# First products of a latent attention: weights split one item ahead, both blocks rotated in one operation, the keys' common part on GpSimd, another order

## The chip, the cores and the metric

The kernel runs on one core of a Trainium2 chip. The metric is the device time of one execution in microseconds. The core's engines work side by side, each through its own queue in order: TensorE (PE, with its weight loads as PEld), VectorE (DVE), ScalarE (ACT), GpSimd (POOL) and SyncE (SP), which here only issues transfers. Semaphores order the engines among each other.

## The reference, cut to what matters

The program is a two-layer block of mixers, cross attention and MLPs on a sequence of 256 tokens with 1024 features, followed by a second block: a latent attention, an expert stage (64 experts), a pool mixer and a second expert stage. The change lies in the latent attention (and in a few lines at the head of the expert stages):

```python
def mla_mixer(x, cos, sin, w_in, q_norm, w_uq, kv_norm, w_ukv, w_o):
    lat = x @ w_in                                         # 256 + 128 + 32 columns
    c_q = rms_norm(lat[..., :Q_LORA_RANK], q_norm)
    c_kv = rms_norm(lat[..., Q_LORA_RANK:Q_LORA_RANK + KV_LORA_RANK], kv_norm)
    k_rope = apply_rope(lat[..., Q_LORA_RANK + KV_LORA_RANK:], cos, sin)
    q = (c_q @ w_uq).reshape(B, S, N_HEADS, QK_NOPE_DIM + QK_ROPE_DIM)   # 16 heads, 64 + 32
    q_nope = q[..., :QK_NOPE_DIM]
    q_rope = apply_rope(q[..., QK_NOPE_DIM:], cos[:, :, None, :], sin[:, :, None, :])
    kv = (c_kv @ w_ukv).reshape(B, S, N_HEADS, QK_NOPE_DIM + V_HEAD_DIM)
    k_nope, v = kv[..., :QK_NOPE_DIM], kv[..., QK_NOPE_DIM:]
    # causal softmax attention of q_nope, q_rope on k_nope, k_rope, then
    return o @ w_o
```

The rotation of each head's 32 columns is x1*cos - x2*sin and x2*cos + x1*sin on halves of 16. The keys have one rotated part for all heads.

## The kernel before, in words

**Weights.** All weights come through one list of items in the order of use, 1 MB or a little less each. `issue` (L170 to L188) starts a transfer into the next slot of a ring of ten; SyncE issues it, eight early items of the expert stage go through GpSimd's queue. In the expert stages thirteen more slots come in. The products of the first half work in a split form: `split_steps` (L225 to L241) has ScalarE copy an item's high part (`wh`, L236) and VectorE subtract to get the low part (`wl`, L239), in two halves, and both take slots of the same ring. A product with a split weight is three matmul passes: (high, high), (low weight, high), (high, low input). `w(key)` (L243 to L251) hands out the next item and decides how far ahead items are split and issued at that point; `tick` splits one half of an item where the program calls it. The items of the latent attention are lat0, lat1, uq0, ukv0, uq1 and the output weights mo0 to mo3.

**The latent attention, `mla`.** Tokens lie in two blocks of 128 (`b`). The order on every engine is the order in which the program is written. First the latent product (PE, L285), the evacuation `lat` with the row scale (ACT, L1170), transposes (PE, L1175), the transposed latents' high part `cTh` (ACT, L1177) and low part `cTl` (DVE, L1178), sums of squares (ACT, L1182), the inverse root of four columns on VectorE (L1184, L373 to L377: one start, three rounds) giving `rr`, and the scale of the queries `rqs` (DVE, L1188). Then `rope` (L1198 to L1209), six operations on VectorE for one block: for the keys' common part (`kr`, copied into `ka`, `kb`, `kc` at L1232) and at the end of `uq(i)` for eight heads of queries. `uq(i)` (L1211 to L1224) is 24 matmuls into four PSUM banks, which ScalarE evacuates with `rqs` (L1221). `ukv(j)` (L1236 to L1246) is the product for four heads' keys and values: keys evacuated by ScalarE (L1245), values by VectorE (L1246). `pre(p)` transposes queries and keys of two heads (PE, L1255) and copies them out, one head on VectorE (L1258), one on ScalarE (L1260). `scores(p)` (L1266, L1267) and the softmax (row bound on VectorE L443, exponential on ScalarE L455, normalization on VectorE L463, L467) follow; `att.main` runs the pairs of heads with the output product (L322).

**What stands between.** After the first two pairs' scores, `bc(10)` (L1032) broadcasts a gain vector through TensorE into two PSUM banks, VectorE multiplies x by row scale and gain (L1293, four operations of 128x512), the output weights mo0 are split by four ticks, and `uq(1)` follows. The product with x into the accumulator (L1300) opens the main loop. `moe` begins with copies of the accumulator into x (ACT L1363, DVE L1364), with statistics (L1366, L1371) for the norm.

## Time and profile before

| what | value |
|---|---|
| time, median of 3 runs | 1840.31 us (1839.34 to 1840.73) |
| the profiled execution's own time | 1839.08 us |
| its span | 1837.3 us |
| mean granted TensorE clock | 0.960 |
| TensorE busy | 1645.4 us (90%) |
| VectorE busy | 763.4 us (42%) |
| ScalarE busy | 576.6 us (31%) |
| GpSimd busy | 12.5 us (1%), 27 instructions |
| moved by DMA | 550.11 MB, 299 GB/s over the span |

The page cuts the span into 40 slices of 46 us. The latent attention lies in slices 18 and 19; the expert stages and the pool mixer are the slices behind it. In the timeline a row is a start, a duration, an engine, a line, the operation with its operands and shape; an `x4` behind it groups four consecutive ones, with their summed time; in brackets stands how long the engine was idle before and what released it.

### The profile page before, as it was taken

The numbers are of one execution on the slowest core, as the hardware profiler recorded it, in microseconds if no ns is written. First come the engines' busy times: TensorE is split into PE (matmuls) and PEld (weight loads), VectorE is DVE, ScalarE is ACT, GpSimd is POOL, SyncE is SP. The second block draws the span as 40 slices with busy tenths as digits, with TensorE's granted clock in tenths as the row PEclk, the third lists the DMA queues.
The fourth block names the chain that finished last, engine by engine and source line by source line (L and its number), as shares of the span: only waits on it lengthen the run. The fifth ranks groups of instructions, "written<-read, shape, count | busy, mean of one in ns | idle before, by whom it ended". The sixth has DMA issues, their size and how long they took to land.

```text
span 1837.3 us, 29848 instructions
## 1 busy us (share of the span) xinstructions
PE 1645.4 (90%) x12682; PEld 1200.0 (65%) x12682; DVE 763.4 (42%) x1582; ACT 576.6 (31%) x1043; POOL 12.5 (1%) x27
## 2 busy tenths in 40 slices
PE   7999999999999999999998778878799977987876
PEld 7998899999878899987754344434366434443433
DVE  6886476555676565568521121111043202110102
ACT  5545454444465454456411100000022100000001
POOL 0000000000000000000000000000000000000000
PEclk9999999999999999999999988988999998988899
DMA  8543455555534355546899999999999999999996
GB/s 299 177 161 116 131 175 198 184 185 181 184 115 136 118 186 189 192 151 248 319 416 426 426 426 425 426 426 426 420 426 425 426 426 426 426 424 426 426 426 255
DMA packets 128902, 550.11 MB, mean 299 GB/s; under 512 B 10891, under 2 KB 32883, under 8 KB 80499
## 3 DMA queue, kind: packets, MB, share of 16 engines
q1 hardware_dynamic: 127107, 539.27, 75.0%
q0 software_dynamic: 1216, 8.39, 1.2%
q8 instruction: 103, 1.69, 0.3%
q10 hardware_dynamic: 432, 0.39, 0.1%
q14 instruction: 44, 0.36, 0.1%
HBM read 546.98 MB, written 1.05 MB: 298 GB/s over the span
## 4 chain that ended last, share of the span: by engine, by line
PE 50%; DMA 45%; DVE 3%; ACT 2%; issue 1%; SPq 0%; ACTq 0%; DVEq 0%
DMA wr<-in_moe_w 44%; PE a L322 16%; PE b L306 9%; PE a L306 6%; PE a L285 3%; PE b L763 3%; PE a L763 2%; PE b L1497 2%; PE b L486 1%; PE b L1465 1%; PE b L475 1%; PE b L346 1%; PE b L801 1%; DMA wr<-in_xa_w_kv 1%; PE b L734 1%; PE b L828 1%
## 5 line engine op out<-in xcount | busy, mean ns | idle before, releaser
L1497 PE MATMUL b<-wr,xg 128*32 128x256 f32 x4096 | 307.0, 426 | 107.9 <-DMA wr<-in_moe_w 107.9
L239 DVE TENSOR_TENSOR wl<-wr,wh 128x1024 fp32r<-128x1024 f32 (+4 forms) x268 | 309.8, 1198 | 115.3 <-ACT wh L236 67.6
L1497 PEld LDWEIGHTS b<-wr,xg 128*32 128x32 f32 x4096 | 148.9, 122 | 272.9 <-DMA wr<-in_moe_w 146.4
L236 ACT ACTIVATE wh<-wr 128x1024 fp32r<-128x1024 f32 (+4 forms) x268 | 265.1, 1037 | 99.9 <-DVE wl L239 72.0
L1501 DVE SCALAR_TENSOR_TENSOR th<-th,b 128x256 f32<-128x256 f32 x32 | 13.5, 421 | 482.3 <-ACT th L1500 482.3
L1500 ACT ACTIVATE th<-b 128x256 f32<-128x256 f32 x32 | 12.3, 384 | 520.8 <-PE b L1497 520.8
L322 PE MATMUL a<-wh,yh 128*128 128x512 f32 x416 | 169.0, 406 | 0.0
L322 PE MATMUL a<-wh,yl 128*128 128x512 f32 x416 | 164.6, 396 | 0.6 <-DVE yl L337 0.6
L322 PE MATMUL a<-wl,yh 128*128 128x512 f32 x416 | 164.0, 394 | 0.0
L1465 PE MATMUL b<-G,x 128*128 128x128 f32 x1024 | 132.3, 290 | 19.4 <-DVE G L1447 10.5
L1524 PE MATMUL b<-wr,hT 128*32 128x512 f32 x992 | 124.7, 601 | 27.7 <-ACT hT L1512 23.2
L1465 PEld LDWEIGHTS b<-G,x 128*128 128x128 f32 x1024 | 126.0, 204 | 32.9 <-issue 17.3
L306 PE MATMUL b<-xh,wl 128*128 128x256 f32 x448 | 121.9, 282 | 0.0
L306 PE MATMUL b<-xh,wh 128*128 128x256 f32 x448 | 121.8, 281 | 0.0
L1533 PE MATMUL a<-Y,GT 128*128 128x512 f32 x248 | 116.9, 614 | 0.0
L306 PE MATMUL b<-xl,wh 128*128 128x256 f32 x448 | 110.4, 282 | 0.0
L1524 PEld LDWEIGHTS b<-wr,hT 128*32 128x32 f32 x992 | 32.7, 110 | 99.0 <-issue 51.2
L322 PEld LDWEIGHTS a<-wh,yl 128*128 128x128 f32 x416 | 78.1, 188 | 20.2 <-DVE yl L337 1.4
L1533 PEld LDWEIGHTS a<-Y,GT 128*128 128x128 f32 x248 | 42.0, 189 | 75.2 <-issue 29.7
L322 PEld LDWEIGHTS a<-wh,yh 128*128 128x128 f32 x416 | 78.1, 188 | 19.7 <-issue 3.0
L322 PEld LDWEIGHTS a<-wl,yh 128*128 128x128 f32 x416 | 78.3, 188 | 17.1
L306 PE MATMUL a<-xh,wh 128*128 128x256 f32 x320 | 88.8, 287 | 0.1
(467 smaller groups left out, 2468.9 us busy)
## 6 DMA issues: line engine op xcount, KB each, us to landing
wr<-in_moe_w SPq DMA_DIRECT2D x368, 1024.0 KB, 19.6
wr<-in_mlp_w_up SPq DMA_DIRECT2D x32, 1024.0 KB, 5.3
wr<-in_mlp_w_down SPq DMA_DIRECT2D x32, 1024.0 KB, 4.8
wr<-in_xa_w_kv SPq DMA_DIRECT2D x16, 1024.0 KB, 5.8
wr<-in_xa_w_q SPq DMA_DIRECT2D x8, 1024.0 KB, 5.0
wr<-in_xa_w_o SPq DMA_DIRECT2D x8, 1024.0 KB, 4.8
wr<-in_cd_w_in SPq DMA_DIRECT2D x8, 1024.0 KB, 5.0
wr<-in_moe_w POOLq DMA_DIRECT2D x8, 1024.0 KB, 6.6
```

Source lines behind the costliest of these rows:

```text
L236: nc.scalar.activation(hi[:, s], r[:, s], AF.Copy)
L239: nc.vector.tensor_tensor(lo[:, s], r[:, s], hi[:, s].bitcast(F32), op=ALU.subtract)
L285: nc.tensor.matmul(outs[b][j], xT(a, h * 4 + kk)[:, b * 128:(b + 1) * 128], wt[c][:, kk, j * n:(j + 1) * n], start=(h == 0 and kk == 0 and ...
L306: nc.tensor.matmul(o[f // 2][:, f % 2, :], wt[c][:, kk, f * 128:(f + 1) * 128], xT(a, h * 4 + kk), start=(h == 0 and kk == 0 and a == 0 an ...
L322: nc.tensor.matmul(acc[b][hf], yT[a][:, chunk, b * 128:(b + 1) * 128], wt[c][:, j, hf * 512:(hf + 1) * 512], start=(first and a == 0 and c ...
L346: nc.tensor.transpose(ps[k // 2][:, k % 2, b * 128:(b + 1) * 128], x[:, b, k * 128:(k + 1) * 128], self.ident)
L475: nc.tensor.transpose(ps[:, o:o + 128], s[:, o:o + 128], self.ident)
L763: nc.tensor.matmul(o[:, f], lt, rt, start=(k == 0 and f == 0 and a == 0 and c == 0), stop=(k == 7 and c == 1), skip_group_check=True)
L1465: nc.tensor.matmul(ps[:, k], xk[:, b, 4 * i + k], Gf[:, b], start=(b == 0), stop=(b == 1))
L1497: nc.tensor.matmul(ps[32 * e:32 * e + 32, which], xg[:, k, 32 * e:32 * e + 32], w(e, k), start=(which == 0 and k == 0), stop=(k == 7), ski ...
L1524: nc.tensor.matmul(y[hf][32 * e:32 * e + 32], hT[:, c, 32 * e:32 * e + 32], w(c)[:, hf * 512:(hf + 1) * 512], start=(c == 0), stop=(c == 1 ...
L1533: nc.tensor.matmul(acc[b][hf], GT[:, b * 128:(b + 1) * 128], Y[:, hf * 512:(hf + 1) * 512], start=first, stop=end, skip_group_check=True)
```

## The change

The diff touches five places. `w()` splits one item less far ahead at lat1 and uq0, finishes an item that is half split when it is asked for, and issues one transfer less at one point. In `mla`, the gain broadcast moves right behind the evacuation of the latents, and the multiplication of x between the inverse root and the query scale. `rope` takes an engine and both blocks at once, 256 elements per partition for eight heads; the keys' part runs on GpSimd, and the queries' rotation becomes `turned_q(i)`, called after `ukv(0)` and after `uq(1)`. The values of the second block are evacuated by ScalarE. The products are called in another order, the four ticks stand once before and once behind `uq(1)`. In `moe` the first statistics stand behind both copies.

```diff
--- before.py
+++ after.py
@@ -245,9 +245,11 @@
         assert self.items[i][0] == key, (self.items[i][0], key)
         self.w_next += 1
         if self.w_split <= i or not self.attending:
-            self.split(i + (0 if i == 0 else 1 if i < 3 else 3 if key == ("lat", 1) else 2))
+            self.split(i + (0 if i == 0 else 1 if i < 3 or key in (("lat", 1), ("uq", 0)) else 2))
+        elif self.part is not None and self.w_split == i + 1:
+            self.split(i)
         left = self.n_split - i
-        self.issue(self.n_split + {4: 3, 3: 4, 2: 5, 1: 7}[left] if left < 5 else i + 2 + self.depth)
+        self.issue(self.n_split + {4: 3, 3: 4, 2: 5, 1: 7}[left] if left < 5 else i + 2 + self.depth - (left == 6))
         return self.sp.pop(i)
 
     def step(self):
@@ -1168,6 +1170,7 @@
             lat = ap.tile([128, 2, 416], F32, name="lat")
             for b in range(2):
                 nc.scalar.activation(lat[:, b], o[b][0], AF.Copy, scale=rs[:, b:b + 1])
+            gain = self.bc(10)
             cT = [ap.tile([128, 3, 256], F32R, name=n) for n in ("cTh", "cTl")]
             for c in range(3):
                 ps = self.pb([128, 256])
@@ -1184,6 +1187,11 @@
                 nc.vector.tensor_scalar(t, t, 1.0 / n, 1e-6, op0=ALU.mult, op1=ALU.add)
             self.rsqrt(rr, 4)
             rk = rr[:, 2:4]
+
+            for b in range(2):
+                for h in range(2):
+                    t = x[:, b, h * 512:(h + 1) * 512]
+                    nc.vector.scalar_tensor_tensor(t, t, rs[:, b:b + 1], gain[h], op0=ALU.mult, op1=ALU.mult)
             rqs = ap.tile([128, 2], F32, name="rqs")
             nc.vector.tensor_scalar(rqs, rr[:, 0:2], -(96.0 ** -0.5), None, op0=ALU.mult)
 
@@ -1195,18 +1203,23 @@
             qk = [ap.tile([96, 2, 256], F32, name=f"qkT{i}") for i in range(4)]
             va, vb = ap.tile([128, 2, 8, 64], F32, name="va"), ap.tile([128, 2, 4, 64], F32, name="vb")
 
-            def rope(dst, src, nh, b):
-                x1, x2 = src[:, :, 0:16], src[:, :, 16:32]
-                cos = cs[:, 0, b, None, :].to_broadcast([128, nh, 16])
-                sin = cs[:, 1, b, None, :].to_broadcast([128, nh, 16])
-                t = self.cc(C_SWA, 256).rearrange("p (h d) -> p h d", d=32)[:, :nh]
-                u = ru[:, :nh]
-                nc.vector.tensor_tensor(t[:, :, 0:16], x1, cos, op=ALU.mult)
-                nc.vector.tensor_tensor(t[:, :, 16:32], x2, cos, op=ALU.mult)
-                nc.vector.tensor_tensor(u[:, :, 0:16], x2, sin, op=ALU.mult)
-                nc.vector.tensor_tensor(u[:, :, 16:32], x1, sin, op=ALU.mult)
-                nc.vector.tensor_tensor(dst[:, :, 0:16], t[:, :, 0:16], u[:, :, 0:16], op=ALU.subtract)
-                nc.vector.tensor_tensor(dst[:, :, 16:32], t[:, :, 16:32], u[:, :, 16:32], op=ALU.add)
+            def rope(eng, dst, src, t, u):
+
+                nh = src.shape[2]
+                x1, x2 = src[:, :, :, 0:16], src[:, :, :, 16:32]
+                cos, sin = (cs[:, i, :, None, :].to_broadcast([128, 2, nh, 16]) for i in range(2))
+                eng.tensor_tensor(t[:, :, :, 0:16], x1, cos, op=ALU.mult)
+                eng.tensor_tensor(t[:, :, :, 16:32], x2, cos, op=ALU.mult)
+                eng.tensor_tensor(u[:, :, :, 0:16], x2, sin, op=ALU.mult)
+                eng.tensor_tensor(u[:, :, :, 16:32], x1, sin, op=ALU.mult)
+                eng.tensor_tensor(dst[:, :, :, 0:16], t[:, :, :, 0:16], u[:, :, :, 0:16], op=ALU.subtract)
+                eng.tensor_tensor(dst[:, :, :, 16:32], t[:, :, :, 16:32], u[:, :, :, 16:32], op=ALU.add)
+
+
+            kr, kt_, ku_ = (ap.tile([128, 2, 1, 32], F32, name=n) for n in ("kr", "krt", "kru"))
+            rope(nc.gpsimd, kr, lat[:, :, None, 384:416], kt_, ku_)
+            for k, n in ((ka, 8), (kb, 4), (kc, 4)):
+                nc.gpsimd.tensor_copy(k[:, :, :, 64:96], kr.to_broadcast([128, 2, n, 32]))
 
             def uq(i):
                 wt = self.w("uq", i)
@@ -1219,18 +1232,13 @@
                                                  start=(k == 0 and a == 0 and c == 0), stop=(k == 1 and a == 1))
                         h = 8 * i + 4 * j
                         nc.scalar.activation(qt[h // 4][:, b].rearrange("p h d -> p (h d)"), o, AF.Copy, scale=rqs[:, b:b + 1])
-                for b in range(2):
-                    t = (qa, qb)[i][:, b, :, 64:96]
-                    rope(t, t, 8, b)
-            ru = ap.tile([128, 8, 32], F32, name="ru")
+
+            def turned_q(i):
+                t = (qa, qb)[i][:, :, :, 64:96]
+                rope(nc.vector, t, t, *ru)
+            ru = [ap.tile([128, 2, 8, 32], F32, name=n) for n in ("rt", "ru")]
             vc = ap.tile([128, 2, 4, 64], F32, name="vc")
             v = [(va, 0), (va, 4), (vb, 0), (vc, 0)]
-            for b in range(2):
-                t = ap.tile([128, 1, 32], F32, name="kr", bufs=2)
-                rope(t, lat[:, b, None, 384:416], 1, b)
-                for k, n in ((ka, 8), (kb, 4), (kc, 4)):
-                    nc.vector.tensor_copy(k[:, b, :, 64:96], t.to_broadcast([128, n, 32]))
-
             uq(0)
             self.attend_on()
             wt = self.w("ukv", 0)
@@ -1243,7 +1251,11 @@
                                          start=(a == 0 and c == 0), stop=(a == 1))
                     ov = o.rearrange("p (h d) -> p h d", d=128)
                     nc.scalar.activation(kt[j][:, b, :, 0:64], ov[:, :, 0:64], AF.Copy, scale=rk[:, b:b + 1])
-                    nc.vector.tensor_scalar(v[j][0][:, b, v[j][1]:v[j][1] + 4], ov[:, :, 64:128], rk[:, b:b + 1], None, op0=ALU.mult)
+                    vd = v[j][0][:, b, v[j][1]:v[j][1] + 4]
+                    if b:
+                        nc.scalar.activation(vd, ov[:, :, 64:128], AF.Copy, scale=rk[:, b:b + 1])
+                    else:
+                        nc.vector.tensor_scalar(vd, ov[:, :, 64:128], rk[:, b:b + 1], None, op0=ALU.mult)
             QK = {}
 
             def pre(p):
@@ -1277,23 +1289,21 @@
             att = self.attend(ap, 8, scores, lambda h, kb: v[h // 4][0][:, kb, v[h // 4][1] + h % 4], lambda h: mask, outp,
                                     lambda p: (ys[p // 4][0][:, p % 4], ys[p // 4][1][:, p % 4]), pre=pre)
             ukv(0)
+            turned_q(0)
             ukv(1)
+            ukv(2)
             pre(0)
-            ukv(2)
+            ukv(3)
             pre(1)
-            ukv(3)
             att.pro(0)
             att.pro(1)
             att.soft2(0)
-
-            g = self.bc(10)
-            for b in range(2):
-                for h in range(2):
-                    t = x[:, b, h * 512:(h + 1) * 512]
-                    nc.vector.scalar_tensor_tensor(t, t, rs[:, b:b + 1], g[h], op0=ALU.mult, op1=ALU.mult)
             for _ in range(4):
                 self.tick()
             uq(1)
+            turned_q(1)
+            for _ in range(4):
+                self.tick()
             acc = self.pacc()
             for b in range(2):
                 for h in range(2):
@@ -1362,12 +1372,10 @@
         for b in range(2):
             nc.scalar.activation(half_x(b, 0), by8(y[b][0]), AF.Copy)
             nc.vector.tensor_copy(half_x(b, 1), by8(y[b][1]))
-            if b == 0:
-                nc.vector.bn_stats(st[:, 0, 0], y[0][0])
         for b in range(2):
             for k in range(8):
                 nc.tensor.transpose(pt[b][k // 4][:, k % 4], xk[:, b, k], self.ident)
-        for b, h in ((0, 1), (1, 0), (1, 1)):
+        for b, h in ((0, 0), (0, 1), (1, 0), (1, 1)):
             nc.vector.bn_stats(st[:, b, h], y[b][h])
         for b in range(2):
             for i in range(2):
```

VectorE's queue from the end of the inverse root (`rr` is its result, `rqs` the scale of the queries, `kr` the keys' rotated part, `qa` the first eight heads of queries, `cst`, `ru` and `rt` room for the rotation). Before:

```order
L377 SCALAR_TENSOR_TENSOR rr<-nwt,nwy 128x4
L1188 TENSOR_SCALAR rqs<-rr 128x2
L1204 TENSOR_TENSOR cst<-lat,cs 128x16
L1205 TENSOR_TENSOR cst<-lat,cs 128x16
L1206 TENSOR_TENSOR ru<-lat,cs 128x16
L1207 TENSOR_TENSOR ru<-lat,cs 128x16
L1208 TENSOR_TENSOR kr<-cst,ru 128x16
L1209 TENSOR_TENSOR kr<-cst,ru 128x16
L1232 COPY ka<-kr 128x8x32
L1232 COPY kb<-kr 128x4x32
L1232 COPY kc<-kr 128x4x32
```

The same place in the changed kernel:

```order
L379 SCALAR_TENSOR_TENSOR rr<-nwt,nwy 128x4
L1194 SCALAR_TENSOR_TENSOR x<-x,rs,b 128x512 x4
L1196 TENSOR_SCALAR rqs<-rr 128x2
L239 TENSOR_TENSOR wl<-wr,wh 128x1024 x2
L1258 TENSOR_SCALAR va<-a,rr 128x256
L1211 TENSOR_TENSOR rt<-qa,cs 128x16x16
L1212 TENSOR_TENSOR rt<-qa,cs 128x16x16
L1213 TENSOR_TENSOR ru<-qa,cs 128x16x16
L1214 TENSOR_TENSOR ru<-qa,cs 128x16x16
L1215 TENSOR_TENSOR qa<-rt,ru 128x16x16
L1216 TENSOR_TENSOR qa<-rt,ru 128x16x16
```

The multiplications of x now stand ahead of the scale, the low halves of the key/value weights behind it, and the keys' rotation is gone from this queue.

ScalarE's queue around the second query product, from the last exponential of the first pairs (`qb` the second eight heads of queries, `pt` transposed probabilities). Before:

```order
L455 ACTIVATE s,den<-s,mn 128x256
L1260 ACTIVATE qkT_7896<-b 96x512
L236 ACTIVATE wh<-wr 128x1024 x2
L1221 ACTIVATE qb<-a,rqs 128x384 x4
L477 ACTIVATE pt<-b 128x384 x2
```

The same place in the changed kernel:

```order
L457 ACTIVATE s,den<-s,mn 128x256
L1272 ACTIVATE qkT_7898<-b 96x512
L236 ACTIVATE wh<-wr 128x768 x2
L1234 ACTIVATE qb<-a,rqs 128x384 x4
L236 ACTIVATE wh<-wr 128x1024 x2
L479 ACTIVATE pt<-b 128x384 x2
```

The halves of 1024, the output weights mo0, moved behind the query evacuation; in their place stand halves of 768, the weights of the second query product itself.

## Rows read from the trace of the kernel before

**Rows 1.** The page's rate strip: GB/s in 40 equal slices of the span.
```profile
GB/s 299 177 161 116 131 175 198 184 185 181 184 115 136 118 186 189 192 151 248 319 416 426 426 426 425 426 426 426 420 426 425 426 426 426 426 424 426 426 426 255
```

**Rows 2.** Windows: span, length, busy us of PE, PEld, DVE, ACT, POOL, clock, DMA, GB/s.
```profile
840.00:860.00 20.00, 19.77 (x124) 16.30 (x123) 17.95 (x68) 15.04 (x45) 1.06 (x2) 1.00 0.64 258
860.00:880.00 20.00, 20.00 (x127) 15.91 (x126) 13.35 (x49) 13.78 (x42) 1.06 (x2) 1.00 0.32 115
880.00:900.00 20.00, 20.00 (x115) 14.86 (x114) 9.29 (x27) 10.09 (x24) 1.31 (x4) 1.00 0.90 349
```

**Rows 3.** Timeline of the transfer issues on SyncE's and GpSimd's queues: start, us, queue, operation.
```profile
899.71 3.50 SPq L182 DMA_DIRECT2D wr<-in_moe_w  x7
...
822.45 1.09 POOL L182 DMA_DIRECT2D wr<-in_moe_w  x2 [355.96 <-ACT wh L236]
```

**Rows 4.** Waits of PE from 820 to 860: us in total, times, longest.
```profile
PE b L1255 <- DVE qa L1209: 1.0, 1, 1.0
PE b L1175 <- ACT lat L1170: 0.9, 2, 0.8
PE a L1218 <- DVE cTl L1178: 0.8, 1, 0.8
```

**Rows 5.** Timeline around the second query product (L1218).
```profile
842.07 1.95 PE L1032 MATMUL b<-brow,keep 128*128 128x128 f32 x16
...
843.77 0.42 PE L1218 MATMUL a<-wh,cTh 128*128 128x384 f32 x1
...
844.00 2.72 DVE L1293 SCALAR_TENSOR_TENSOR x<-x,rs,b 128x512 f32<-128x512 f32 x4
844.00 1.99 ACT L236 ACTIVATE wh<-wr 128x1024 fp32r<-128x1024 f32 x2
```

**Rows 6.** Timeline of the first products, from the splits to the queries' rotation.
```profile
821.05 4.10 DVE L239 TENSOR_TENSOR wl<-wr,wh 128x1024 fp32r<-128x1024 f32 x4
...
823.70 1.20 ACT L1177 ACTIVATE cTh<-b,col 128x256 fp32r<-128x256 f32 x3 [0.42 <-PE b L1175]
...
828.92 0.17 DVE L1188 TENSOR_SCALAR rqs<-rr 128x2 f32<-128x2 f32 x1
...
829.18 2.00 ACT L1221 ACTIVATE qa<-a,rqs 128x384 f32<-128x384 f32 x4 [2.47 <-DVE rqs L1188]
...
829.82 0.50 PE L1242 MATMUL a<-wh,cTh 128*128 128x512 f32 x1
...
831.30 0.29 DVE L1204 TENSOR_TENSOR cst<-qa,cs 128x128 f32<-128x128 f32 x1
```

**Rows 7.** Timeline: TensorE's first head transposes.
```profile
834.11 0.32 PE L1255 MATMUL b<-keep,qa 128*96 128x128 f32 x1 [0.96 <-DVE qa L1209]
```

**Rows 8.** Chain of waits, 805 to 905: the third key/value product's piece (start, us).
```profile
835.09 1.38 PE a L1242 x6
```

**Rows 9.** Timeline: the product with x, and VectorE's copy behind the second normalization.
```profile
848.07 3.59 PE L1300 MATMUL a<-x,keep 128*128 128x512 f32 x8
...
853.23 0.69 DVE L1258 COPY qkT<-b 96x512 f32<-96x512 f32 x1 [0.44 <-PE b L1255]
```

**Rows 10.** Groups by line on GpSimd: busy us, mean ns of one.
```profile
L1735 POOL TENSOR_TENSOR Y<-Y,x 128x512 f32<-128x512 f32 x2 | 3.2, 1592 | 480.0 <-ACT Y L1733 479.9
L1360 POOL TENSOR_SCALAR r_i<-keep 128x32 f32<-128x32 f32 x4 | 1.2, 289 | 0.2
```

**Rows 11.** Timeline: the first statistics of the expert stage.
```profile
899.77 0.70 DVE L1366 BATCH_NORM_STATS2 n_st<-a 128x6 f32<-128x512 f32 x1 [0.15 <-PE a L322]
```

**Rows 12.** Timeline: TensorE after a wait in the first mixer.
```profile
39.31 0.39 PE L285 MATMUL a<-wh,xh 128*128 128x260 f32 x1 [3.13 <-DVE gate L573]
```

**Rows 13.** Windows behind that wait, columns as in rows 2.
```profile
39.50:40.00 0.50, 0.29 (x2) 0.09 (x1) 0.50 (x2) 0.50 (x2) 0.00 (x0) 0.68 1.11 354
40.00:41.00 1.00, 1.00 (x5) 1.00 (x6) 0.93 (x3) 1.00 (x4) 0.00 (x0) 0.50 1.10 346
...
44.00:45.00 1.00, 0.00 (x0) 0.00 (x0) 1.00 (x4) 1.00 (x2) 0.00 (x0) 1.00 0.60 125
```

## The prediction

> **What bounds the kernel now.** I began with the page's strip of rates over the span. From about the twentieth of its 40 slices the memory side moves some 426 GB/s without a break [rows 1]. So the second half (the two expert stages) is bound by transfers; what happens before it counts by when it lets those transfers start. The busy table by stretches answers that: from 860 to 880 us TensorE is busy for 20.00 of 20 us while the DMA share is 0.32, and from 880 to 900 it has risen to 0.90 [rows 2]. The issue list says what it waits for: seven weight items go out together at 899.71 [rows 3], the moment at which the latent attention frees its ring slots. Until then the ring is full, after it the DMA share never drops. **A microsecond added to the latent attention before 899.7 therefore reaches the end nearly whole**, as does one saved.
>
> Inside that stage TensorE waits little: 1.0 us for the rotated queries, 0.9 for the evacuated latents, 0.8 for the low half of the transposed latents [rows 4]. These three are the whole of its waits there, so little can be won. The changed lines sit between 821 and 859 us.
>
> **The change part by part.** All sums are on the profiled execution, 1839.08 us, whose span is 1837.3; the median of the three runs, 1840.31, is 1.23 above it, and I add that at the end.
>
> *Front (821 to 829).* The gain broadcast moves from before the second query product to right behind the latent product. There it ran from 842.07 to the next product at 843.77, 1.70 us [rows 5]. Put at 821.91, when the latent product is through, it ends at 823.6. The transposes start behind it; two of them, some 0.5 us, lie ahead of ScalarE's first copy of them, which today starts at 823.70 [rows 6] and becomes 824.1. Most of the broadcast hides under the latents' evacuation; **0.4 us sticks out**. The VectorE's four low-half operations (4.10 us from 821.05 [rows 6]: two of 1024 and two of 768 elements, so 1.17 and 0.88 us each) are no longer there, because the splits now run one item ahead. That removes the 0.8 wait for the low half. But the first query product ends the same 0.5 us earlier and meets the next wait, so nothing of it reaches the end.
>
> *The scale of the queries.* Now to the step that decides. VectorE's queue held: inverse root, query scale (828.92), key rotation, query rotation from 831.30 [rows 6]. It will hold: inverse root, the four multiplications of x by its gain, query scale. These four took 2.72 us [rows 5]. They used to stand where VectorE had time; now ScalarE's four query evacuations, which already wait 2.47 us for the scale [rows 6], wait for them too. The scale comes 0.4 + 2.72, less a small overlap, **3.04 us later**, at 831.96. TensorE cannot go round it: the first key/value product takes a PSUM bank that the first evacuation frees (it started 0.90 behind the scale, at 829.82 [rows 6]), so it starts at 832.86, and TensorE, finished with the queries at 829.2, stands still for **3.6 us**.
>
> *Rotation.* Twelve operations of 128 elements at a spacing of 0.20 us become six of 256. Their shape is not in the trace. The spacing cannot be under 0.20 nor over 0.40 (no saving); between 16 elements and 128 an operation grows by about 1.07 ns per element (0.29 us at 128 [rows 6]), which gives 0.334, and I take 2.17 us with the first latency, against 2.6 now. With the two low halves of the key/value weights (2.34 us) and a value copy ahead of it in the queue, the rotation ends at 837.36. The head transposes, today at 834.11 behind a wait of 0.96 for the rotation [rows 7], start at 837.4, **+3.3**. The third key/value product (1.38 us [rows 8]) now stands before them, inside that wait, so the scores are later by only 3.3 - 1.4 = **+1.9**.
>
> *The second query product.* Without the broadcast it could start at 843.77 + 1.9 - 1.70 = 844.0. But its own weights are now split right ahead of it. ScalarE comes to that behind eight exponentials and a copy: what stood there at 844.00 (two halves, 1.99 us [rows 5]) starts at 845.9. The first half, 768 elements, takes 0.75; the product's first instruction goes at 846.65, its second after the low half at 847.55, its fifth after the second low half at 848.4, and the twenty left at 4.30/24 = 0.179 us end at 852.0. The product with x, now at 848.07 [rows 9], follows: **+3.9**. TensorE idles 2.6 us, then 0.7 and 0.5.
>
> *Behind it.* VectorE then runs the rotation (from 852.75, 2.17), the low halves of the first output weights (2.34) and the normalization of the second pair (1.2), and only then the copy that stands at 853.23 [rows 9]: 858.45, **+5.2**. The main loop hangs on that copy, and TensorE is full from there on.
>
> *Key rotation on GpSimd.* Six operations of 2x16 elements and copies of 512, 256 and 256. Its nearest rows: 289 ns for 32 elements, 1592 ns for a product of 512 [rows 10]. So 1.7 us for the six; the copies lie between 0.3 each and 1.6 + 0.9 + 0.9, all in 2.6 to 5.1 us. From 823.3 that ends between 826 and 828.4; the copies are needed at 837.4. At nothing, then, under 9 us of cover. Queued behind them are GpSimd's weight transfers: the two at 822.45 [rows 3] go out 4 to 6 us later, while the ring's later slots come free only after 848; nothing.
>
> *Value copies to ScalarE, expert head.* Four copies of about 0.5 us leave VectorE for ScalarE, which waits there anyway: nothing. In the expert head the first statistics (0.70 us at 899.77 [rows 11]) leave the way of the copy behind it: **-0.3** at the most.
>
> Sum of the waits: 5.2 - 0.3 = **+4.9 us**, 1844.0 on the profiled execution, 1845.2 as a median.
>
> *The clock.* At 39.31 us TensorE resumes after a wait of 3.13 us [rows 12], and right behind it the granted clock is 0.68, then 0.50 (its 1.2 GHz level instead of 2.4), while the gap of over a microsecond at 44 to 45 leaves it at 1.00 [rows 13]. In the latent stage, from 840 on, it is 1.00 [rows 2]. My idle of 3.6 us lies above the first row; 2.6 us between the two. A fall of about 3.3 us at half speed costs 1.6 us at the first place; at the second, where the product is partly waiting anyway, 1.3. I take the first and leave out the second, by the row it is nearer to: **+1.5**. Forecast 1839.08 + 4.9 + 1.5 + 1.23 = **1846.7**.
>
> **Rivals.**
> - *No fall of the clock*: both gaps too short or too broken. 1845.2, from 1843.5 to 1846.
> - *Both gaps make it fall*, with a third, some 2 us before 859, as a candidate: 4.9 + 1.6 + 1.3, up to 9: 1848 to 1850.
> - *The waits are partly swallowed*: the +3.9 and +5.2 share an origin; if ScalarE reaches the split of the second query weights earlier (its exponentials are paced by VectorE, which loses four copies and the x products here), and the loop regains a microsecond of the rest, +1 to +3 remains: 1840 to 1843.5. Against it: TensorE is full from 860 on, so there is no slack to regain time in.
> - *Faster*: the relief outweighs the scale. TensorE sheds the 0.8 and 1.0 waits [rows 4], 1.3 of the broadcast, 0.4 before the key/value product and 0.3 in the head, 3.8 in all, to 1836.5. It decides by one point: the x products must end before the scale would have come, by 829. For it: VectorE loses 4.10 us of splits there. Against it: they stand behind the inverse root, whose start is set by ScalarE's squares and not by VectorE.
> - *GpSimd meets VectorE*: if the two engines' operations block each other, the key rotation lies at the inverse root (827 to 829) and lengthens it. It costs at most GpSimd's own 3.3 us: 1848 to 1850, with a later start 1852. Today nothing but transfers' issues runs on GpSimd there, so no row bears on it.
>
> On the last, the Trainium skill, "SBUF — State Buffer", § Who interferes with whom, says that a VectorE instruction with two SBUF inputs contends with a GpSimd instruction that reads SBUF; the inverse root and the low halves have two such inputs. "GPSIMD Engine Reference", § 2.1 Instruction dispatch, adds a first call of about 6 us that shows no instruction; as an estimate by that page GpSimd would end at some 834, still before 837.4, but then beside the root and the x products. No row shows either. By these rules the sum would be 0 to 3.3 us higher; I keep the lower.
>
> **How the numbers follow.** One fall 0.36 (1845.8 to 1847.6); no fall 0.22; more falls 0.18; swallowed 0.10; faster 0.09; GpSimd 0.05. The range 1843.0 to 1850.5 holds the first three but for a sliver, and a part of the swallowed and the GpSimd cases: 0.8. A measurement of this kernel tells about 0.2% from no change, 3.7 us, so "same" is 1836.6 to 1844.0: 0.10 and the low end of "no fall", 0.15. Slower 0.76, faster 0.09.
>
> **What would show it.** In the changed profile: ScalarE's query evacuations wait over 4 us for the scale, near 832; the first key/value product starts near 832.9 behind an idle of 3 to 4 us and the granted clock drops to 0.50 behind it or doesn't; the head transposes start near 837.4 and wait for the rotation, not for GpSimd's key copies; the second query product waits some 2.6 us for the high half of its weights; the seven transfers go out near 905 to 906. I am wrong if the scale comes before 830, if the second query product finds its weights ready, or if the transfers of 899.71 move by less than the x product does.

## The result, and the profile after

The changed kernel takes 1851.8 us (median of 6 runs, 1847.06 to 1853.16) against 1840.88 us before (6 runs, 1839.34 to 1841.77): a ratio of 1.0057, 95% interval 1.0046 to 1.0067. It is slower, as forecast, but by 10.9 us where 6.4 were forecast, and the time lies above the range of 1843.0 to 1850.5. The profiled execution took 1852.76 us with a span of 1850.9.

The two executions are compared here by distances from the start of the last matmul of the latent product, because they arrive there at different times for reasons ahead of the change (at 821.72 before, at 823.50 after). First the timeline of the changed kernel from that matmul to the first key/value product: start, duration, engine, line, operation, and in brackets the idle time ahead and its releaser.

```profile
823.50 0.35 PE L287 MATMUL a<-wh,xl 128*128 128x416 f32 x1
...
823.69 1.95 PE L1034 MATMUL b<-brow,keep 128*128 128x128 f32 x16
...
825.47 0.60 PE L1178 MATMUL b<-keep,lat 128*128 128x128 f32 x4
...
825.89 0.84 ACT L1180 ACTIVATE cTh<-b,col 128x256 fp32r<-128x256 f32 x2 [1.34 <-PE b L1178]
...
826.94 0.44 PE L1178 MATMUL b<-keep,lat 128*128 128x128 f32 x2 [0.87 <-DVE cTl L1181]
...
829.73 0.17 DVE L1187 TENSOR_SCALAR rr<-rr 128x2 f32<-128x2 f32 x1 [0.70 <-ACT junk L1185]
...
831.80 2.71 DVE L1194 SCALAR_TENSOR_TENSOR x<-x,rs,b 128x512 f32<-128x512 f32 x4
834.43 0.16 DVE L1196 TENSOR_SCALAR rqs<-rr 128x2 f32<-128x2 f32 x1
834.50 2.35 DVE L239 TENSOR_TENSOR wl<-wr,wh 128x1024 fp32r<-128x1024 f32 x2
834.69 2.00 ACT L1234 ACTIVATE qa<-a,rqs 128x384 f32<-128x384 f32 x4 [3.09 <-DVE rqs L1196]
835.32 0.80 PE L1250 MATMUL a<-wh,cTh 128*128 128x512 f32 x1 [3.73 <-ACT qa L1234]
```

The scale comes 10.93 behind the last latent matmul, against 7.20 in [rows 6]. The multiplications of x stand ahead of it and take 2.71 us, as read in [rows 5], and TensorE stands still for 3.73 us ahead of its first key/value matmul. One row is new: the third pair of transposes waits 0.87 us for VectorE's `cTl`. Next the second query product and what follows:

```profile
850.32 1.56 ACT L236 ACTIVATE wh<-wr 128x768 fp32r<-128x768 f32 x2
...
851.21 0.69 PE L1231 MATMUL a<-wh,cTh 128*128 128x384 f32 x1 [2.41 <-ACT wh L236]
...
852.20 0.69 PE L1231 MATMUL a<-wl,cTh 128*128 128x384 f32 x1 [0.30 <-DVE wl L239]
...
858.80 3.60 PE L1310 MATMUL a<-x,keep 128*128 128x512 f32 x8
...
861.76 2.35 DVE L239 TENSOR_TENSOR wl<-wr,wh 128x1024 fp32r<-128x1024 f32 x2
...
865.16 0.68 DVE L1270 COPY qkT<-b 96x512 f32<-96x512 f32 x1
```

The product waits 2.41 us for the high half of its own weights. The product with x is 9.0 us later against the last latent matmul than in [rows 9], the copy behind the low halves 10.2. The windows show what lies between these waits (span, length, busy us of PE, PEld, DVE, ACT, POOL, then granted clock, DMA share, GB/s):

```profile
828.00:832.00 4.00, 3.59 (x21) 3.27 (x19) 2.51 (x14) 3.50 (x10) 0.39 (x1) 1.00 0.86 303
832.00:836.00 4.00, 0.68 (x2) 0.52 (x3) 4.00 (x7) 1.31 (x3) 0.00 (x0) 0.72 0.86 316
836.00:840.00 4.00, 4.00 (x11) 3.13 (x11) 3.28 (x8) 2.41 (x6) 0.00 (x0) 0.50 0.89 327
...
848.00:852.00 4.00, 1.49 (x9) 0.83 (x6) 3.19 (x11) 3.89 (x13) 0.00 (x0) 0.85 0.00 0
852.00:856.00 4.00, 3.80 (x12) 3.76 (x13) 1.01 (x2) 0.58 (x1) 0.00 (x0) 0.50 0.00 0
```

Behind both idle stretches the granted clock stands at 0.50 (1.2 GHz), where [rows 2] had 1.00. The records of the clock give 6.8 us of it from 833.8 and 6.8 us from 850.8. SyncE's seven transfers of [rows 3] now go out at 911.53:

```profile
911.53 3.44 SPq L182 DMA_DIRECT2D wr<-in_moe_w  x7
```

From the last latent matmul to there are 88.0 us, 10 more than before. Until the last latent matmul the profiled execution after is 1.8 us late; that start differs by 2.2 us between two executions of one and the same kernel below (821.91 and 824.08), so it can't be put down to the change.

### The profile page after: what moved, and what is told of

Same layout as the page of the kernel before. It is cut to its first block, busy times and chain, and to the rows that moved or that the text cites. A ratio compares the mean times of both kernels' runs of the same rounds, so it can differ in the third digit from the quotient of the medians.

```text
span 1850.9 us, 29828 instructions
## 1 busy us (share of the span) xinstructions
PE 1654.6 (89%) x12682; PEld 1205.2 (65%) x12682; DVE 758.7 (41%) x1548; ACT 578.4 (31%) x1047; POOL 15.1 (1%) x36
## 4 chain that ended last, share of the span: by engine, by line
PE 58%; DMA 35%; DVE 4%; ACT 2%; issue 1%; SPq 0%; ACTq 0%; DVEq 0%
DMA wr<-in_moe_w 34%; PE a L324 16%; PE b L308 9%; PE a L308 6%; PE b L1505 5%; PE a L287 4%; PE b L765 3%; PE b L1473 3%; PE a L765 2%; PE b L1532 2%; PE a L1541 1%; PE b L488 1%; PE b L348 1%; PE b L477 1%; DVE wl L239 1%
```

## The experiments

The table holds, for each profiled execution, starts in the timeline less the start of the last latent matmul, in us: the scale of the queries, the first key/value matmul, the first scores, the first matmul of the second query product, the product with x, VectorE's copy of rows 9, and the first transpose of the expert head, which closes the stage; and the falls of the granted clock inside it. The first line is what the prediction's sum gives, without its term for the clock. Each kernel but one (a_rest and rest_again) was profiled once, so a difference between two lines is one execution against one.

```
kernel            scale  kv     scores  query2  x       copy    stage   falls of the clock
predicted sum     10.24  11.14  18.75   24.93   30.2    36.7    82.9
before             7.20   8.10  16.85   22.05   26.34   31.50   78.04   none
after             10.93  11.82  21.64   27.71   35.30   41.66   88.10   6.8 + 6.8
a_warm            10.93  11.82  19.45   25.52   31.00   37.36   83.70   none
a_warm_first      10.94  11.83  19.44   25.52   32.54   38.90   85.29   3.4 (second)
a_bank            10.14  11.02  20.88   26.95   34.58   40.93   87.33   6.8 + 6.8
a_swap             8.41   9.31  21.14   27.21   34.22   40.57   86.96   3.4 + 3.4
a_undo_x           6.70   7.60  15.23   21.30   29.94   36.29   82.70   3.4 (second)
a_undo_splits     11.42  12.30  21.25   24.67   28.96   34.23   80.76   3.4 (first)
a_rest             7.42   9.37  16.63   21.84   26.13   31.29   77.82   3.4 (first product)
rest_again         7.41   8.31  15.91   21.11   25.40   30.57   77.04   none
c_halves           7.42   8.32  15.97   19.39   23.70   28.95   75.48   none
c_dve_keys         7.19   8.09  17.24   20.65   24.94   30.21   76.71   none
```

**The theory after the result.** Each of two reorderings makes TensorE wait, for the scale and for its own weights, and each wait makes the clock fall; the rest of the change costs nothing. The rivals: the rest (GpSimd, the order of products) has a part in the loss; or the time beyond my sum of waits is something other than the clock.

**One part undone: the broadcast and the multiplications of x.**

```diff
-            gain = self.bc(10)
             cT = [ap.tile([128, 3, 256], F32R, name=n) for n in ("cTh", "cTl")]
...
-            for b in range(2):
-                for h in range(2):
-                    t = x[:, b, h * 512:(h + 1) * 512]
-                    nc.vector.scalar_tensor_tensor(t, t, rs[:, b:b + 1], gain[h], op0=ALU.mult, op1=ALU.mult)
             rqs = ap.tile([128, 2], F32, name="rqs")
...
             att.soft2(0)
+            gain = self.bc(10)
+            for b in range(2):
+                for h in range(2):
+                    t = x[:, b, h * 512:(h + 1) * 512]
+                    nc.vector.scalar_tensor_tensor(t, t, rs[:, b:b + 1], gain[h], op0=ALU.mult, op1=ALU.mult)
```

> The changed kernel with one part undone: the gain broadcast and the four multiplications of x stand behind the second normalization again, as before. My theory now: of the some 10 us lost, the first place costs 4 (scale of the queries 3.7 later, of which 2.7 are the four multiplications and the rest the two PSUM banks that the broadcast holds) and a fall of the clock there some 2 more. Expected: the query evacuations no longer wait over 3 us for the scale, the first fall of the clock (at 834 in the changed kernel's profile) is gone, and the head transposes start at or before the time of the kernel before. But the multiplications now stand between the normalization and the low halves of the second query weights, so that product waits for the low halves instead: some 5 us later at the product with x, perhaps with the second fall. Time +4 to +7.5 over the kernel before. Rival, that the loss comes from the parts that stay here (GpSimd's rotation, the merged rotation, the order): +9 to +11, as the changed kernel.

Measured: 1845.71 us against 1841.23, ratio 1.0021 (1.0012 to 1.0031). The first wait and fall are gone: the scale stands at 6.70, the scores at 15.23. The product with x is 3.6 us later than before, where some 5 were expected. TensorE's waits from 815 to 870 (line waited for: us in total, times, longest) show the new one at the second query product:

```profile
PE a L1226 <- DVE wl L239: 2.6, 1, 2.6
```

It waits for the low half, which queues behind the multiplications of x, and the second fall (3.4 us) stays. So the multiplications can't simply go back: with weights split just ahead of their use they stand in somebody's way in either place.

**The other part undone: the splits and the ticks.**

```diff
-            self.split(i + (0 if i == 0 else 1 if i < 3 or key in (("lat", 1), ("uq", 0)) else 2))
-        elif self.part is not None and self.w_split == i + 1:
-            self.split(i)
+            self.split(i + (0 if i == 0 else 1 if i < 3 else 3 if key == ("lat", 1) else 2))
...
-        self.issue(self.n_split + {4: 3, 3: 4, 2: 5, 1: 7}[left] if left < 5 else i + 2 + self.depth - (left == 6))
+        self.issue(self.n_split + {4: 3, 3: 4, 2: 5, 1: 7}[left] if left < 5 else i + 2 + self.depth)
...
             turned_q(1)
-            for _ in range(4):
-                self.tick()
```

> The changed kernel with its other part undone: weights split as far ahead as before, and the four ticks before the second query product only. My theory: the first wait (some 3.7 us for the scale) and the first fall of the clock stay; the second wait (2.4 us for the high half) and the second fall go, and so does the low half of the output weights in front of the second normalization. By the sum at the second query product: head transposes +6, scores +4.8, the broadcast's 1.7 no longer ahead of it, product with x +3. Time +2.5 to +4 over the kernel before. Rival, that the first place alone makes the loss: +8 or more.

Measured: 1845.0 us, ratio 1.0017 (1.0008 to 1.0026). The first wait stays (3.7 us, scale at 11.42) with a fall of 3.4 us; the second is gone, and from scores to the product with x the kernel makes up a part of what it had lost: scores 4.4 behind the kernel before, product with x 2.6 behind. The stage is 2.7 us longer.

**Both undone**, so that only the merged rotation, GpSimd's part, ScalarE's value copies, the order of the products and the expert head stay. Its diff is the two above together.

> Both parts undone; what stays of the change: one rotation for both blocks, keys' part on GpSimd, the second block's values evacuated by ScalarE, the order of the key/value products, the expert head. My theory: none of these costs anything; the wait of 1.0 us for the rotation goes, and the rotation after the second query product is 0.4 shorter: -0.5 to -1.5 against the kernel before. Rival, that GpSimd's operations hold up VectorE or that ScalarE is overloaded: +1 to +3.

Measured: 1842.11 us, ratio 0.9998 (0.9989 to 1.0007): no difference that can be told. The interval ends at +1.3 us, so of the rival of +1 to +3 only the lowest edge is left; the gain of 0.5 to 1.5 is not shown in the time. In this profile the clock fell once, in the first query product, as the windows show:

```profile
824.00:828.00 4.00, 2.14 (x11) 1.04 (x9) 4.00 (x6) 3.55 (x9) 2.28 (x4) 0.99 0.63 195
828.00:832.00 4.00, 3.99 (x14) 4.00 (x15) 3.29 (x15) 1.25 (x7) 2.90 (x8) 0.59 0.95 326
```

TensorE is idle there for about half of the first window, in three waits of a microsecond and less that the kernel before has too, without a fall in its profile. So this kernel was run once more.

> The same kernel as the one with both parts undone, looked at once more. In its first profile the granted clock fell for 3.4 us in the first query product, behind waits that are also in the kernel before, where it did not fall. If this is chance, it is absent or elsewhere here, and the stage from the last latent matmul to the expert head is 1 to 2 us shorter than the kernel before's 78.0 us; if the parts that stay bring it about, it is there again.

Measured in a single run: 1840.48 us; no fall in the stage, which is 77.04 us long, 1.0 less than before. Whether short waits like these bring a fall differs between two executions of the same program; what decides it stays open.

**The idle stretches filled.** In both, matmuls that write to a bank nobody reads:

```diff
+            self.warm(16)
             ukv(0)
...
+            self.warm(10)
             uq(1)
```

> The changed kernel with 16 and 10 matmuls on the identity, whose result nobody reads, in TensorE's two idle stretches (before the first key/value product and before the second query product). They lie inside the waits (1.78 us for eight of the broadcast, so some 3.6 and 2.2 us). If the granted clock falls because TensorE stood still, both falls of 6.8 us are gone and with them 4 to 5 us: +6 over the kernel before, with the waits for the scale and for the high half as long as in the changed kernel. If the clock is not the cause of what lies beyond my sum of waits, the time stays at +10 to +11.

Measured: 1845.48 us, ratio 1.0023 (1.0014 to 1.0032). The windows at the two places, from its trace:

```profile
832.00:836.00 4.00, 3.84 (x28) 3.25 (x28) 4.00 (x6) 1.92 (x5) 0.00 (x0) 1.00 0.77 288
...
852.00:856.00 4.00, 4.00 (x17) 2.84 (x16) 1.29 (x4) 3.06 (x5) 0.53 (x1) 1.00 0.24 39
```

The clock stays at 1.00, and the stage is 4.4 us shorter than in the changed kernel, although the waited-for operations come just as late (scale 10.93, first key/value matmul 11.82 in both). That separates the two halves of the loss: **5.7 us are waits, 4.4 us are the clock.** Over the kernel before the time is 4.2 us longer by the ratio, less than the 6 expected. Against the changed kernel it fell by 6.3, more than the stage; in the profiles of this study the stretch behind the stage took between 936.3 us (here) and 939.8. The only kernel with two profiles had 939.6 and 939.7 there, so a part of that may belong to the kernel; the remainder isn't explained.

With the first stretch alone filled:

> The changed kernel with the 16 idle matmuls in the first idle stretch only. Theory: each fall of the clock comes from the idle stretch ahead of it and has its own price: the first fall is gone (head transposes at 16.3 behind the last latent matmul, as with both stretches filled, against 18.5), the second stays, 3.4 or 6.8 us long, and the stage is 85 to 86.2 us, between 83.70 with both filled and 88.10 with none. Rival, that filling one stretch is enough: 83.7.

Measured in a single run: 1847.11 us; scores at 19.44, as with both filled, and a fall of 3.4 us behind the second wait, 85.29 for the stage. Each fall belongs to the wait ahead of it, and one of 3.4 us costs 1.6 us at the second place. A fall of 6.8 us cost 2.2 us at the first place (scores at 21.64 in the changed kernel, 19.45 with the wait filled) and the other 2.2 of the 4.4 us at the second.

**The bank.** The third transpose of the latents taken from the other PSUM pool:

```diff
-                ps = self.pb([128, 256])
+                ps = self.pa(256) if c == 2 else self.pb([128, 256])
```

> The changed kernel, but the third transpose of the latents goes into a bank of the other PSUM pool, so that it need not wait until VectorE has emptied one of the two banks that the gain broadcast leaves. My theory: that wait (0.9 us) is the part of the scale's delay that my sum lacked; the scale comes 0.7 to 0.8 earlier behind the latent product (10.1 to 10.2 us behind its last matmul, against 10.93 in the changed kernel and 7.20 before), and with it the first key/value product (near 11.1). Both idle stretches stay, so one or two falls of the clock too. Rival, that the delay comes from the broadcast's own time: 10.9 stays.

Measured in a single run: scale at 10.14, first key/value matmul at 11.02, 0.8 earlier each, and the stage is 0.8 shorter. Both falls of 6.8 us stay (1850.89 us).

**The order of two lines.**

```diff
+            rqs = ap.tile([128, 2], F32, name="rqs")
+            nc.vector.tensor_scalar(rqs, rr[:, 0:2], -(96.0 ** -0.5), None, op0=ALU.mult)
             for b in range(2):
                 for h in range(2):
                     t = x[:, b, h * 512:(h + 1) * 512]
                     nc.vector.scalar_tensor_tensor(t, t, rs[:, b:b + 1], gain[h], op0=ALU.mult, op1=ALU.mult)
-            rqs = ap.tile([128, 2], F32, name="rqs")
-            nc.vector.tensor_scalar(rqs, rr[:, 0:2], -(96.0 ** -0.5), None, op0=ALU.mult)
```

> The changed kernel with one line moved: the scale of the queries ahead of the four multiplications of x, with nothing else changed. If it were only the order of these two, the loss at the first place would be gone (scale 8.2 us behind the last latent matmul, head transposes some 2.7 earlier). My theory: the low halves of the key/value weights then stand behind the multiplications instead, so the product's first matmul goes at 9.1, its second at some 12.3, as in the changed kernel (12.4); head transposes and everything later as in the changed kernel within 0.5 us, but for falls of the clock.

Measured in a single run, 1849.47 us. TensorE's timeline at the first two key/value matmuls:

```profile
832.68 0.50 PE L1250 MATMUL a<-wh,cTh 128*128 128x512 f32 x1 [1.22 <-ACT qa L1234]
835.77 0.66 PE L1250 MATMUL a<-wl,cTh 128*128 128x512 f32 x1 [2.58 <-DVE wl L239]
```

The scale came 2.5 us earlier, the first matmul too, and the second waits the 2.58 us for the low half behind the multiplications: scores at 21.14 against 21.64. Putting the scale first moves the wait by one instruction. (Its two falls were 3.4 us long each instead of 6.8. By the prices above, 1.6 against 2.2 us, that accounts for the 1.1 us by which the stage is shorter; it wasn't tested by itself.)

**A version that is faster than both.** From the kernel with both parts undone, the broadcast in two halves inside TensorE's waits at the front, the third transpose in the other pool, and the multiplications behind the scale; there they are harmless, since the weights have been split long before.

```diff
+            gain = []
+
+            def half(j):
+                gain.append(self.pb([128, 512]))
+                for c in range(4):
+                    nc.tensor.matmul(gain[j][:, c * 128:(c + 1) * 128],
+                                     self.ident[:, 80 + 4 * j + c:81 + 4 * j + c].to_broadcast([128, 128]), self.brow,
+                                     start=True, stop=True)
+
+            half(0)
             cT = [ap.tile([128, 3, 256], F32R, name=n) for n in ("cTh", "cTl")]
...
-                ps = self.pb([128, 256])
+                ps = self.pa(256) if c == 2 else self.pb([128, 256])
...
+            half(1)
             rr = self.sm.tile([128, 4], F32, name="rr")
...
             nc.vector.tensor_scalar(rqs, rr[:, 0:2], -(96.0 ** -0.5), None, op0=ALU.mult)
+            for b in range(2):
+                for h in range(2):
+                    t = x[:, b, h * 512:(h + 1) * 512]
+                    nc.vector.scalar_tensor_tensor(t, t, rs[:, b:b + 1], gain[h], op0=ALU.mult, op1=ALU.mult)
...
-            gain = self.bc(10)
-            for b in range(2):
-                for h in range(2):
-                    t = x[:, b, h * 512:(h + 1) * 512]
-                    nc.vector.scalar_tensor_tensor(t, t, rs[:, b:b + 1], gain[h], op0=ALU.mult, op1=ALU.mult)
```

> The parts that cost nothing (rotation of both blocks, keys' part on GpSimd, values on ScalarE, order, expert head, with the splits of the kernel before), and the gain broadcast in two halves inside TensorE's two waits at the front (behind the latent product, and behind the transposes), the third transpose in the other PSUM pool, and the multiplications of x behind the scale of the queries, ahead of VectorE's first value copy. Theory: scale within 0.3 us of before, head transposes some 1 us later than the order alone would give, the second query product 1.5 to 2.5 earlier than before since neither the broadcast nor the multiplications stand there, and the latent attention 2 to 3 us shorter: 1838 to 1839.5, -0.1 to -0.2%. Rival, that GpSimd or the order costs: 0 to +2 us.

Measured: 1837.49 us against 1840.93, ratio 0.9981 (0.9972 to 0.9990). The stage, counted from the last latent matmul at 822.60, is 2.6 us shorter than before, within the 2 to 3 expected; 1.0 of it the kernel with both parts undone had already (77.04). The time lies just below the 1838 to 1839.5 expected. The head transposes come 0.1 us later than in that kernel (12.81 against 12.74), where 1 was expected. The first key/value matmul waits 0.3 us and not 3.7:

```profile
822.60 0.35 PE L285 MATMUL a<-wh,xl 128*128 128x416 f32 x1
...
830.03 0.17 DVE L1200 TENSOR_SCALAR rqs<-rr 128x2 f32<-128x2 f32 x1
830.11 2.72 DVE L1204 SCALAR_TENSOR_TENSOR x<-x,rs,b 128x512 f32<-128x512 f32 x4
...
830.93 0.50 PE L1258 MATMUL a<-wh,cTh 128*128 128x512 f32 x1 [0.27 <-ACT qa L1242]
...
898.03 3.48 SPq L182 DMA_DIRECT2D wr<-in_moe_w  x7
```

The multiplications run beside the key/value products, and the second query product starts 2.7 us earlier than before, having neither the broadcast ahead of it on TensorE nor the multiplications ahead of it on VectorE.

**GpSimd's part in it.** In this faster version, the keys' rotation back on VectorE:

```diff
-            rope(nc.gpsimd, kr, lat[:, :, None, 384:416], kt_, ku_)
+            rope(nc.vector, kr, lat[:, :, None, 384:416], kt_, ku_)
...
-                nc.gpsimd.tensor_copy(k[:, :, :, 64:96], kr.to_broadcast([128, 2, n, 32]))
+                nc.vector.tensor_copy(k[:, :, :, 64:96], kr.to_broadcast([128, 2, n, 32]))
```

> The faster version (broadcast in two halves, multiplications of x behind the scale) with one part of the change undone: the keys' common part rotated and copied by VectorE, between the multiplications of x and the queries' rotation. Theory: this part is worth something only where VectorE's queue ends last. Here it does (the rotation of the queries releases the head transposes), so the nine operations, some 1.6 to 2 us by the rows of the kernel before, go straight into the head transposes (13.4 to 13.8 us behind the last latent matmul, against 11.84) and into the whole stage (76.0 to 76.5, against 74.51). Rival, that GpSimd's copies were no gain: 11.8 and 74.5 stay.

The 11.84 and 74.51 in this expectation are counted from a point 0.97 us behind the last latent matmul; from the matmul itself the faster version has 12.81 and 75.48, and the forecast reads 14.4 to 14.8 and 77.0 to 77.5.

Measured in a single run: 1839.5 us, head transposes at 14.07, scores at 17.24 and the stage at 76.71, 1.2 us longer than 75.48. The head transposes wait again:

```profile
PE b L1275 <- DVE qa L1224: 1.1, 1, 1.1
```

So this part is worth 1.2 us once VectorE is what TensorE waits for, by one profile against one. The size was below the 1.6 to 2 expected, for a reason that the two traces show: the nine operations took 1.50 us on VectorE (833.12 to 834.62), but the scale came 0.23 us earlier (7.19 against 7.42). Without GpSimd beside it, the inverse root's first two operations took 0.17 and 0.16 us instead of 0.25 and 0.30. What remains, 1.27, is nearly the 1.26 us by which the head transposes are later.

## Why the prediction was wrong

**What held.** The place, the mechanism and the order of events. The scale behind the multiplications, the first key/value matmul behind the scale, the third product hidden in the wait, the second query product behind its own weights, the copy behind the first output weights: each was in the trace after as the sum had it. Sizes: ScalarE's first copy of the transposes was forecast 0.4 later and came 0.4 later (2.39 behind the last latent matmul, 1.98 in [rows 6]); the rotation's spacing of 0.334 us was 0.33; TensorE's idle 3.6 and 2.6 were 3.73 and 2.41; the step from the product with x to the copy grew by 1.3 in the sum and by 1.2 in the trace. GpSimd's nine operations took 2.66 us, at the low end of 2.6 to 5.1, and nobody waited for them. The three waits of [rows 4] weren't quite the whole, a fourth of 0.2 us stands behind them; nothing hung on it. That the end moves nearly one to one with the stage held too: the stage is 10.06 us longer, the median 10.9 (in the two profiled executions the seven transfers moved by 11.8 us and the span by 13.6).

**The step that failed is the clock's**, "I take the first and leave out the second, by the row it is nearer to: +1.5". It measured 4.4 us (a_warm). Two things were wrong in it. The second wait of 2.4 us, which I put on the side without a fall, brought one; the row of 3.13 us [rows 12] and a single gap of over a microsecond [rows 13] were too far apart to place it, and I should have taken the side that costs, or carried both ends in the forecast. And the length: I took the 3.3 us of the one fall that I had read as the length of a fall. In the changed kernel both lasted 6.8 us; in the variants either 3.4 or 6.8. The price of a fall of 3.4 us was nearly right: 1.6 at the second place (a_warm_first), where the prediction had 1.3; at the first place no pair of runs isolates it. The rival "both gaps make it fall" was the true case; I gave it 0.18 and priced it with falls of half their length.

The trace of the kernel before held more than that one fall. TensorE's timeline there, behind two waits in the expert stages, and a window at each (columns as above):

```profile
1143.51 0.77 PE L1465 MATMUL b<-G,x 128*128 128x128 f32 x2 [4.35 <-DVE G L1447]
...
1142.50:1148.50 6.00, 4.99 (x23) 5.02 (x24) 0.85 (x2) 0.60 (x1) 0.00 (x0) 0.50 1.01 423
...
1299.01 0.91 PE L1497 MATMUL b<-wr,xg 128*32 128x256 f32 x2 [2.04 <-DMA wr<-in_moe_w]
...
1302.00:1306.00 4.00, 4.00 (x44) 1.84 (x40) 0.00 (x0) 0.00 (x0) 0.00 (x0) 0.50 1.01 428
```

Both falls last longer than 3.4 us, 6.8 by the records of the clock, as 14 of the 27 falls in that trace do. So the length could have been read, and a wait of 2.04 us with a fall lies nearer to my 2.6 than the gap at 44 to 45 does (though TensorE had waited 1.2 and 1.8 us shortly ahead of it).

**The waits were 0.8 short**: 5.7 (a_warm) instead of 4.9. The missing term is a PSUM bank. The broadcast keeps two of the four banks of its pool until VectorE has multiplied x, the three transposed latents need three, and so the third waits for VectorE to empty one. In the prediction I counted the broadcast's time on TensorE and not the banks that it holds; a_bank shows the 0.8. With both terms as measured, 4.9 + 0.8 + 4.4, the sum is 10.1, and the stage is 10.06 us longer.

**The range** was too narrow for the same reason: its upper end of 1850.5 lies just above the rival with two falls, 1848 to 1850, priced at about 3.3 us each. The remaining 0.9 us between the stage and the medians lie inside the spread of the stretches ahead of it and behind it.

**The rivals.** "Swallowed" and "faster" are out: TensorE gave nothing back in the rest of the stage (from the copy to the expert head 46.54 us before, 46.44 after), and the relief of the splits (0.8 at the front) was real but stood behind the scale, as a_undo_x shows with its scale 0.5 earlier than before. "GpSimd meets VectorE" does not apply to the changed kernel, where GpSimd is through at 827.30 and the inverse root starts at 829.73; it does to its relatives, below. As for the first call of about 6 us that the Trainium skill names for a freshly loaded kernel ("GPSIMD Engine Reference", § 2.1 Instruction dispatch): here GpSimd had run only fills and transfers up to then, and its first operation started at 824.64, some 0.1 us behind the latents' evacuation that it reads, so it isn't seen at this place.

## What to carry to other kernels

Before an operation is moved ahead in an in-order queue, read who waits for the instruction right behind its new place, and count the PSUM banks that its operands hold there; "VectorE has less to do here now" says neither. Here a wait of TensorE of 2.4 to 3.7 us cost the wait and then a stretch at half clock: put a price on both, with more than one fall read from the trace. To separate the two, fill the wait with matmuls that nobody reads; and work like the broadcast here pays in a wait that is already there, in pieces that fit.

## What the runs showed of the hardware

In the latent attention of these profiles TensorE had nine waits of 2.41 to 3.73 us that were not filled, and with each came a fall of the granted clock to 0.50, during the wait or shortly behind it; the falls lasted 3.4 or 6.8 us with no visible reason for the one or the other. The waits that were filled with matmuls (both in a_warm, the first in a_warm_first) had none. One fall came behind waits of 0.8 us and less, in one of two profiles of that kernel.

GpSimd and VectorE get in each other's way. In the changed kernel GpSimd's first two rotations took 0.25 us each, with VectorE idle. In the faster version, and in the kernel with both parts undone, they lie beside the low halves of the weights, a VectorE subtraction with two inputs in SBUF. GpSimd's timeline in the changed kernel:

```profile
824.64 0.25 POOL L1211 TENSOR_TENSOR krt<-lat,cs 128x32 f32<-128x32 f32 x1 [356.27 <-ACT lat L1172]
824.85 0.25 POOL L1212 TENSOR_TENSOR krt<-lat,cs 128x32 f32<-128x32 f32 x1
```

The timeline of the faster version, with VectorE's four subtractions and the start of its inverse root:

```profile
821.93 4.16 DVE L239 TENSOR_TENSOR wl<-wr,wh 128x1024 fp32r<-128x1024 f32 x4
...
824.25 1.02 POOL L1219 TENSOR_TENSOR krt<-lat,cs 128x32 f32<-128x32 f32 x1 [358.28 <-ACT lat L1170]
825.23 0.97 POOL L1220 TENSOR_TENSOR krt<-lat,cs 128x32 f32<-128x32 f32 x1
826.15 0.25 POOL L1221 TENSOR_TENSOR kru<-lat,cs 128x32 f32<-128x32 f32 x1
...
827.10 0.61 POOL L1230 COPY ka<-kr 128x512 f32<-128x512 f32 x1
...
828.12 0.30 DVE L375 TENSOR_TENSOR nwt<-nwy 128x4 f32<-128x4 f32 x1
...
828.85 0.16 DVE L375 TENSOR_TENSOR nwt<-nwy 128x4 f32<-128x4 f32 x1
```

The same operation takes 1.02 and 0.97 us while a subtraction runs and 0.25 as soon as the last has ended at 826.1. The Trainium skill, "SBUF — State Buffer", § Who interferes with whom, states this rule: a VectorE instruction with two SBUF inputs contends with a GpSimd instruction that reads SBUF. The trace agrees, with 0.7 to 0.8 us of blocking per GpSimd operation. GpSimd can afford it, because its copies are needed some seven microseconds later. VectorE pays a little: the first round of the inverse root lies beside GpSimd's copies (the last ends at 828.40) and one of its operations takes 0.30 us where the next round's takes 0.16; in the kernel with both parts undone and in the faster version the scale comes 0.2 us later than before (7.41 and 7.42 against 7.20), and with the keys' rotation back on VectorE it doesn't (7.19).
